# Probabilities scaled by the reciprocals of their sums on ScalarE instead of on GpSimd

## The chip, the cores and the metric

The kernel runs on one core of one Trainium2 chip. A core has five engines that run side by side, each taking its own instructions in sequence: TensorE (PE in the profile, with its weight loads as PEld), VectorE (DVE), ScalarE (ACT), GpSimd (POOL) and SyncE (SP), which here only issues transfers. They meet at semaphores. Matmuls write into PSUM, a small accumulator memory of which this kernel holds eight banks; everything else lies in on-chip memory (SBUF) or in the device's main memory. The metric is the device time of one launch in microseconds. A time is the median of several runs.

## The reference

One step of a two-layer backbone for 512 latent tokens and 128 context tokens, width 1024, in fp32. Each layer normalises and modulates its input, projects it once into four groups of heads (a short gated convolution, a chunked spatial gate, latent attention, windowed attention), projects their concatenated outputs back, adds that through a gate, and does the same for a squared-ReLU MLP. What the change touches is the softmax of both attentions of the latent tokens, cut here to its core:

```python
# latent attention, 4 heads: 512 queries on 512 + 128 keys
s = jnp.einsum('bqhd,bkhd->bhqk', q_blk, kf) * scale
p = jax.nn.softmax(s, axis=-1)
out = jnp.einsum('bhqk,bkhd->bqhd', p, v)

# windowed attention, 4 heads: a band of blocks, the context, and one sink logit per head
logits = jnp.concatenate([s_band, s_ctx, sink_column(sink, s_band)], axis=-1)
p = jax.nn.softmax(logits, axis=-1)
out = einsum(p[..., :n_band], v_band) + einsum(p[..., n_band:-1], v_ctx)
```

So each row of probabilities is an exponential divided by the sum of its row.

## The kernel before

Tokens are columns: 640 of them, worked on in two halves of 384 and 256. Nearly every matrix product is made of three fp32 matmuls (`mm3`, lines 248 to 250), because each operand is split into a rounded part and the rest: the rounded part is a ScalarE cast and the rest a VectorE subtraction (`split`, lines 253 and 254; for weights lines 239 and 240). ScalarE and VectorE therefore stand behind every operand that is computed in the kernel.

Each layer runs its projections, then windowed attention, then latent attention, then the rest of the output projection, then the MLP. Both attentions go by units of one head and two blocks of 128 queries, eight units each, and each unit has a front and a back:

- *Front of a windowed unit* (`swa_front`): score matmuls into a pair of PSUM banks; on VectorE the row's minimum with the mask (line 756); on ScalarE the exponential with its sum (line 759) and the exponential of the sink (line 761); on VectorE the addition of both (line 762) and the reciprocal (line 763); and the scaling of the probabilities `P` (line 764), on GpSimd. Widths are 384 and 512.
- *Front of a latent unit* (`mla_front`): score matmuls, the maximum on VectorE (line 996), the exponential with its sum on ScalarE (line 997), the reciprocal on VectorE (line 999), and the scaling of `Pm` (line 1000), on GpSimd. The width is 640.
- *Back* (`swa_back`, `mla_back`): TensorE transposes the scaled probabilities (line 244, tile `pt`), `split` makes `PT` or `PTm` of them, TensorE multiplies with the values (lines 793 and 1025, tile `pv`), and ScalarE, VectorE and `split` bring the result into the layer's `y`.

`pairs` writes the front of unit i+1 ahead of the back of unit i, and between the pieces of a back it draws filler from a generator: projection tiles (`fm`) in windowed attention, output tiles (`out`) in latent attention. The context tokens have small units of their own (`sc`, `pc`, `pvc`), and their transposed probabilities are copied by line 823. In the first layer VectorE also does the modulation vectors of later layers (line 174) between these pieces.

The written order is not the final one. A scheduler places the instructions on each engine by its own estimate of when each can start, so that a changed instruction also changes the order around it. Buffers come from rotating pools: two PSUM banks for `pt` and `pv`, two pairs of banks for the scores, five tiles for the probabilities.

Of the kernel before, what the change touches and what calls it, by code (L numbers as in the profile page):

```python
# [13 lines left out]
AF = mybir.ActivationFunctionType  # L14
ALU = mybir.AluOpType
# [41 lines left out]
def step_kernel(ctx, tc, xT, wf, wt, wt3, wo1, wo2, wq, wkvs, wada, wnat, wnat2, vec, rows, fnorm, cvec, cache, kpec,  # L57
                masks, rope_s, rope_q, rope_k, o_y, o_ckv, o_kpe, o_k, o_v):
    nc = tc.nc
# [27 lines left out]
    def nm(s):  # L87
        uid[0] += 1
        return f"{s}_{uid[0]}"
# [9 lines left out]
    def bank2(s="bk2"):  # L99
        return s2.tile([128, 2, 512], F32, tag="s2", name=nm(s))  # L100
# [7 lines left out]
    def tp(shape, s):  # L108
        return pool_p.tile(shape, F32, tag="p", name=nm(s))
# [136 lines left out]
    def mm3(out, lhs, rhs, start, stop, more=False):  # L246

        nc.tensor.matmul(out, lhsT=lhs[0], rhs=rhs[0], start=start, stop=False, skip_group_check=more)  # L248
        nc.tensor.matmul(out, lhsT=lhs[0], rhs=rhs[1], start=False, stop=False, skip_group_check=more)  # L249
        nc.tensor.matmul(out, lhsT=lhs[1], rhs=rhs[0], start=False, stop=stop, skip_group_check=more)  # L250
# [185 lines left out]
    def layer(l, h, next_norm, nxt):  # L436
# [165 lines left out]
        for hd in range(4):  # L602
            if hd % 2 == 0:
# [6 lines left out]
                out=u_t[:, :, d0:d0 + 64], in0=ps[:, :320].rearrange("p (t d) -> p t d", t=5),  # L610
                scalar=vl[:, V_SB + hd:V_SB + hd + 1], in1=u_t[:, :, d0:d0 + 64],
                op0=ALU.add, op1=ALU.mult)
# [122 lines left out]
        def swa_front(i):  # L735
            hq, hf = divmod(i, 2)
            n, g = divmod(hq, 2)
            r = slice(64 * n, 64 * n + 64)
            S = bank2("S")
            P = PS[i] = [tp([128, 512], "P") for _ in range(2)]  # L740
            a = sm.tile([128, 4, 2], F32, tag="as", name=nm("as"))
            for j in range(2):
                c = 2 * hf + j
                k0, kn = RNG[c]
                w = 128 * kn
                if stacked:
                    for t in (kw, kl):
                        nc.tensor.matmul(S[:, j, :w], lhsT=qw[g][:, n, 128 * c:128 * c + 128],
                                         rhs=t[:, n, 128 * k0:128 * k0 + w], start=t is kw, stop=t is kl)
                    continue  # L750
                mm3(S[:, j, :w], (qw[g][r, 0, 128 * c:128 * c + 128], qw[g][r, 1, 128 * c:128 * c + 128]),
                    (kw[r, 0, 128 * k0:128 * k0 + w], kw[r, 1, 128 * k0:128 * k0 + w]), True, True)
            for j in range(2):
                c = 2 * hf + j
                w = 128 * RNG[c][1]
                nc.vector.tensor_tensor_reduce(
                    out=P[j][:, :w], in0=S[:, j, :w], in1=msk[:, MSK[c]:MSK[c] + w], op0=ALU.add, op1=ALU.min,
                    scale=1.0, scalar=nsink[:, hq:hq + 1], accum_out=a[:, 0, j:j + 1])
                nc.scalar.activation(P[j][:, :w], P[j][:, :w], AF.Exp, scale=-1.0, bias=a[:, 0, j:j + 1],
                                     accum_out=a[:, 1, j:j + 1])  # L760
                nc.scalar.activation(a[:, 2, j:j + 1], a[:, 0, j:j + 1], AF.Exp, bias=sink[:, hq:hq + 1])
                nc.vector.tensor_add(a[:, 1, j:j + 1], a[:, 1, j:j + 1], a[:, 2, j:j + 1])
                nc.vector.reciprocal(a[:, 3, j:j + 1], a[:, 1, j:j + 1])
                nc.gpsimd.tensor_scalar(out=P[j][:, :w], in0=P[j][:, :w], scalar1=a[:, 3, j:j + 1], scalar2=1.0,
                                        op0=ALU.mult, op1=ALU.mult)
            yield

        def swa_back(i):
# [216 lines left out]
        def mla_front(i):  # L985
            hd, hf = divmod(i, 2)
            ke, qq = kk[hd % 2], qqs[hd]
            P = PS[i] = [tp([128, TOK], "Pm") for _ in range(2)]
            a = sm.tile([128, 4, 2], F32, tag="as", name=nm("as"))
            for j in range(2):  # L990
                c = 2 * hf + j
                S = bank2("S")
                for z in range(2):
                    mm3(S[:, z, :320], (qq[:, 0, 128 * c:128 * c + 128], qq[:, 1, 128 * c:128 * c + 128]),
                        (ke[:, 0, 320 * z:320 * z + 320], ke[:, 1, 320 * z:320 * z + 320]), True, True)
                nc.vector.tensor_reduce(out=a[:, 0, j:j + 1], in_=S[:, :, :320], op=ALU.max, axis=AX.XY, negate=True)
                nc.scalar.activation(P[j].rearrange("p (a b) -> p a b", a=2), S[:, :, :320], AF.Exp,
                                     bias=a[:, 0, j:j + 1], accum_out=a[:, 1, j:j + 1])
                nc.vector.reciprocal(a[:, 3, j:j + 1], a[:, 1, j:j + 1])
                nc.gpsimd.tensor_scalar(out=P[j], in0=P[j], scalar1=a[:, 3, j:j + 1], scalar2=1.0,  # L1000
                                        op0=ALU.mult, op1=ALU.mult)
                yield

        def mla_back(i):
# [78 lines left out]
        def load_up():  # L1083
# [5 lines left out]
        s_ = side()  # L1089
        next(s_)  # L1090
        pairs([swa_front(i) for i in range(7)] + [swa_ctx_front(), swa_front(7)],
              [swa_back(i) for i in range(7)] + [swa_ctx_back(), swa_back(7)], s_, C1)
        run(s_)
# [15 lines left out]
        def second():  # L1109
            run(mla_k(1))  # L1110
            run(q_pair(1))
            yield from mla_front(4)

        s_ = side2()
        pairs([mla_front(i) for i in range(4)] + [second(), mla_front(5), mla_ctx_front(), mla_front(6), mla_front(7)],
              [mla_back(i) for i in range(6)] + [mla_ctx_back(), mla_back(6), mla_back(7)], s_, C2)
        run(s_)
# [370 lines left out]
```

## Time and profile before

| | |
|---|---|
| median of 3 runs | 1513.88 us (1511.9 to 1515.99) |
| profiled execution | 1513.0 us, span 1510.8 us |
| TensorE busy | 1461.8 us, 97% |
| VectorE busy | 1133.2 us, 75% |
| ScalarE busy | 694.7 us, 46% |
| GpSimd busy | 79.3 us, 5% |
| granted TensorE clock, mean | 0.988 of full speed |

The busy shares are means over the whole span. The edited lines run in four stretches only: windowed attention at about 126 to 208 us and 865 to 940 us, latent attention at about 230 to 310 us and 962 to 1040 us. Buffer numbers are left out in the profile's names (`P`, `Pm`) and stand in the order's (`P_2104`).

### The profile page before, as it was taken

Reading aid. Unit: us, or ns where it says so; the run is one execution under the profiler, and the core shown is the slowest. Engines: PE = TensorE matmul, PEld = TensorE weight load, DVE = VectorE, ACT = ScalarE, POOL = GpSimd, SP = SyncE. Lnnn points to the kernel's source line nnn. Section 1 sums busy time; section 2 is a strip of 40 time slices with the busy share of each in tenths; the row PEclk is TensorE's granted clock in tenths of the full one; section 3 lists DMA queues with packets and bytes.
Section 4 is the critical chain, followed back from the end, with each engine's and each line's share of the span. In section 5 each row is a group of like instructions: output and inputs, shape, how many; then the busy total and the mean of one; then the engine's idle time right before and its main releaser. Section 6 shows DMA issues by size and latency. Waiting matters only on the chain.

```text
span 1510.8 us, 24974 instructions
## 1 busy us (share of the span) xinstructions
PE 1461.8 (97%) x9700; PEld 1405.1 (93%) x9700; DVE 1133.2 (75%) x2297; ACT 694.7 (46%) x1469; POOL 79.3 (5%) x103
## 2 busy tenths in 40 slices
PE   6999999999999999999999999999999999999997
PEld 3898989899999999999999998998999999999996
DVE  5998888889977867875477676887977666567656
ACT  4644556746233232233246455775826334324431
POOL 0011102200000000000000121110000000000000
PEclk9999999999999999999999999999999999999998
DMA  9643311324655444443112411022123123222312
GB/s 346 205 153 127 96 56 58 96 87 153 194 161 161 155 144 150 153 153 127 64 49 75 134 43 44 22 71 67 57 78 104 57 84 98 70 70 85 96 45 71
DMA packets 50422, 160.87 MB, mean 106 GB/s; under 512 B 6272, under 2 KB 10368, under 8 KB 50304
## 3 DMA queue, kind: packets, MB, share of 16 engines
q1 hardware_dynamic: 48320, 154.68, 31.8%
q10 hardware_dynamic: 1664, 3.93, 0.7%
q8 instruction: 77, 1.26, 0.3%
q0 software_dynamic: 320, 0.66, 0.2%
q14 instruction: 41, 0.34, 0.1%
HBM read 155.55 MB, written 3.05 MB: 105 GB/s over the span
## 4 chain that ended last, share of the span: by engine, by line
PE 81%; DVE 8%; ACT 5%; issue 2%; POOL 1%; DMA 1%; POOLq 0%; DVEq 0%; ACTq 0%
PE w L250 15%; PE w L249 15%; PE w L248 14%; PE tm L250 2%; PE tm L248 2%; PE tm L249 2%; PE qcd L248 2%; PE qcd L250 2%; PE qcd L249 2%; PE out L248 2%; PE fm L248 2%; PE fm L250 2%; PE fm L249 2%; PE out L249 2%; PE out L250 2%
## 5 line engine op out<-in xcount | busy, mean ns | idle before, releaser
L248 PE MATMUL w<-u,hl 128*128 128x384 f32 (+1 forms) x1024 | 315.8, 309 | 1.9 <-DVE x L428 1.2
L249 PE MATMUL w<-u,hl 128*128 128x384 f32 (+1 forms) x1024 | 315.9, 308 | 0.7 <-DVE u L1231 0.7
L250 PE MATMUL w<-u,hl 128*128 128x384 f32 (+1 forms) x1024 | 315.5, 309 | 0.6 <-DVE hl L240 0.6
L239 ACT CAST hl<-raw 128x1024 fp32r<-128x1024 f32 (+3 forms) x176 | 170.7, 972 | 244.0 <-PE w L250 151.4
L240 DVE TENSOR_TENSOR hl<-raw,hl 128x1024 fp32r<-128x1024 f32 (+3 forms) x176 | 199.4, 1135 | 60.6 <-ACT hl L239 59.8
L428 DVE SCALAR_TENSOR_TENSOR x<-w,mod,x 128x128 f32<-128x128 f32 (+1 forms) x384 | 155.4, 434 | 59.4 <-PE w L250 58.1
L248 PEld LDWEIGHTS w<-u,hl 128*128 128x128 f32 x1024 | 193.3, 189 | 3.0 <-DVE x L428 1.4
L249 PEld LDWEIGHTS w<-u,hl 128*128 128x128 f32 x1024 | 193.6, 189 | 1.0 <-DVE u L1231 1.0
L250 PEld LDWEIGHTS w<-u,hl 128*128 128x128 f32 x1024 | 193.4, 189 | 0.8 <-DVE hl L240 0.8
L249 PE MATMUL w<-h,hl 128*128 128x384 f32 (+1 forms) x576 | 178.8, 311 | 0.7 <-DVE h L369 0.6
L248 PE MATMUL w<-h,hl 128*128 128x384 f32 (+1 forms) x576 | 177.8, 311 | 0.4 <-ACT h L365 0.2
L250 PE MATMUL w<-h,hl 128*128 128x384 f32 (+1 forms) x576 | 178.1, 310 | 0.0
L174 DVE CUSTOM_DVE_ANT_0 junk<-adaw,cb,vec 128x1024 f32<-128x1024 f32 x84 | 108.2, 1289 | 30.6 <-DMA adaw<-in_wada 30.5
L249 PEld LDWEIGHTS w<-h,hl 128*128 128x128 f32 x576 | 109.8, 191 | 1.7 <-DVE h L369 1.5
L248 PEld LDWEIGHTS w<-h,hl 128*128 128x128 f32 x576 | 109.6, 191 | 1.4 <-ACT h L365 1.3
L250 PEld LDWEIGHTS w<-h,hl 128*128 128x128 f32 x576 | 109.8, 191 | 0.2
L174 DVE CUSTOM_DVE_ANT_0 adaw<-adaw,cb,vec 128x1024 f32<-128x1024 f32 x84 | 107.9, 1285 | 0.7
L248 PE MATMUL fm<-h,hl 128*128 128x256 f32 (+1 forms) x288 | 91.5, 318 | 0.0
L249 PE MATMUL fm<-h,hl 128*128 128x256 f32 (+1 forms) x288 | 89.7, 311 | 0.0
L250 PE MATMUL fm<-h,hl 128*128 128x256 f32 (+1 forms) x288 | 89.5, 311 | 0.0
L1176 ACT ACTIVATE rr<-w 128x384 f32<-128x384 f32 (+1 forms) x72 | 31.4, 436 | 101.5 <-PE w L250 101.4
L249 PE MATMUL tm<-hl,h 128*128 128x384 f32 (+1 forms) x240 | 77.3, 322 | 0.6 <-DVE hl L240 0.6
(338 smaller groups left out, 3237.1 us busy)
## 6 DMA issues: line engine op xcount, KB each, us to landing
raw<-in_wf SPq DMA_DIRECT2D x146, 512.0 KB, 3.5
adaw<-in_wada SPq DMA_DIRECT2D x84, 512.0 KB, 3.6
raw<-in_wo SPq DMA_DIRECT2D x24, 384.0 KB, 3.1
adan<-in_wnat SPq DMA_DIRECT2D x12, 512.0 KB, 8.2
raw<-in_wt SPq DMA_DIRECT2D x16, 384.0 KB, 4.0
x<-in_xT ACTq DMA_DIRECT2D x4, 640.0 KB, 7.1
raw<-in_wt SPq DMA_DIRECT2D x8, 288.0 KB, 2.8
raw<-in_wo SPq DMA_DIRECT2D x4, 512.0 KB, 3.6
```

Source lines behind the costliest of these rows:

```text
L174: nc.vector.tensor_tensor_reduce(out=raw if g else junk, in0=raw, in1=cb[:, g, :], op0=ALU.mult, op1=ALU.add, scale=1.0, scalar=vecs[l][:, ...
L239: nc.scalar.copy(hl[:, 0, :n], raw[:, :n])
L240: nc.vector.tensor_sub(hl[:, 1, :n], raw[:, :n], f(hl[:, 0, :n]))
L248: nc.tensor.matmul(out, lhsT=lhs[0], rhs=rhs[0], start=start, stop=False, skip_group_check=more)
L249: nc.tensor.matmul(out, lhsT=lhs[0], rhs=rhs[1], start=False, stop=False, skip_group_check=more)
L250: nc.tensor.matmul(out, lhsT=lhs[1], rhs=rhs[0], start=False, stop=stop, skip_group_check=more)
L428: nc.vector.scalar_tensor_tensor(out=x[:, m, t0:t0 + n], in0=ps[:, t0 - b0:t0 - b0 + n], scalar=mods[l][g][:, gate + m:gate + m + 1], in1= ...
L1176: nc.scalar.activation(r, ps[:, :n], AF.Relu)
```

## The change

The multiplication of the probabilities by the reciprocals of their sums becomes a ScalarE copy with a scale per partition. Nothing else is edited.

```diff
@@ swa_front
                 nc.vector.reciprocal(a[:, 3, j:j + 1], a[:, 1, j:j + 1])
-                nc.gpsimd.tensor_scalar(out=P[j][:, :w], in0=P[j][:, :w], scalar1=a[:, 3, j:j + 1], scalar2=1.0,
-                                        op0=ALU.mult, op1=ALU.mult)
+                nc.scalar.activation(P[j][:, :w], P[j][:, :w], AF.Copy, scale=a[:, 3, j:j + 1])
@@ mla_front
                 nc.vector.reciprocal(a[:, 3, j:j + 1], a[:, 1, j:j + 1])
-                nc.gpsimd.tensor_scalar(out=P[j], in0=P[j], scalar1=a[:, 3, j:j + 1], scalar2=1.0,
-                                        op0=ALU.mult, op1=ALU.mult)
+                nc.scalar.activation(P[j], P[j], AF.Copy, scale=a[:, 3, j:j + 1])
```

In the changed kernel the lines behind line 765 count one less, those behind line 1000 two less. The scheduler places instructions differently on TensorE, VectorE and ScalarE, all within the four stretches but for two transfers that change places with a neighbour. The next rows are of ScalarE at the start of windowed attention in the second layer, before; the numbers tell tiles of one name apart.

```order
L759 ACTIVATE P_9199,as_9200<-P_9199,as_9200 128x512
L761 ACTIVATE as_9200<-as_9200,row_8361 128x1
L759 ACTIVATE P_9218,as_9220<-P_9218,as_9220 128x512
L761 ACTIVATE as_9220<-as_9220,row_8361 128x1
L759 ACTIVATE P_9219,as_9220<-P_9219,as_9220 128x384
```

The same place on ScalarE after the change:

```order
L759 ACTIVATE P_9199,as_9200<-P_9199,as_9200 128x512
L761 ACTIVATE as_9200<-as_9200,row_8361 128x1
L759 ACTIVATE P_9218,as_9220<-P_9218,as_9220 128x512
L764 ACTIVATE P_9198<-P_9198,as_9200 128x384
L764 ACTIVATE P_9199<-P_9199,as_9200 128x512
L761 ACTIVATE as_9220<-as_9220,row_8361 128x1
L759 ACTIVATE P_9219,as_9220<-P_9219,as_9220 128x384
```

The two scalings of the first unit stand behind the first exponential of the second unit. ScalarE at the end of windowed attention in the first layer, before (`pc` is the context's probabilities, `sgut` the spatial gate's transposed tile):

```order
L759 ACTIVATE P_2105,as_2106<-P_2105,as_2106 128x384
L761 ACTIVATE as_2106<-as_2106,row_388 128x1
L253 CAST y_1090<-yt_2098 64x256
L823 COPY pc_2019<-ptc_2130 128x512
L684 ACTIVATE y_1086<-sgut_2138 128x384
L684 ACTIVATE y_1086<-sgut_2153 128x256
```

The same place after the change:

```order
L253 CAST y_1090<-yt_2098 64x256
L759 ACTIVATE P_2105,as_2106<-P_2105,as_2106 128x384
L761 ACTIVATE as_2106<-as_2106,row_388 128x1
L764 ACTIVATE P_2104<-P_2104,as_2106 128x512
L822 COPY pc_2019<-ptc_2130 128x512
L684 ACTIVATE y_1086<-sgut_2138 128x384
L764 ACTIVATE P_2105<-P_2105,as_2106 128x384
```

One scaling of the last unit stands ahead of the copy of the context's probabilities, the other behind it. The third place is TensorE at the end of latent attention in the first layer, before: the last two of the ten products of the last unit but one (`pv_3190`), transposes of the last unit (`pt_3209`, `pt_3216`), and output matmuls (`out_3309`) as filler.

```order
L1025 MATMUL pv_3190<-PTm_3170,vm_1097 64x256
L1025 MATMUL pv_3190<-PTm_3170,vm_1097 128x256
L244 MATMUL pt_3209<-ident,Pm_3118 128x128
L244 MATMUL pt_3209<-ident,Pm_3119 128x128
...
L248 MATMUL out_3309<-ymla_2378,hl_3292 128x384
L249 MATMUL out_3309<-ymla_2378,hl_3292 128x384
L250 MATMUL out_3309<-ymla_2378,hl_3292 128x384
L244 MATMUL pt_3216<-ident,Pm_3118 128x128
```

After the change, from the transposes of the last unit but one (`pt_3178`, `pt_3185`) on:

```order
L248 MATMUL out_3309<-ymla_2378,hl_3292 128x384
L249 MATMUL out_3309<-ymla_2378,hl_3292 128x384
L244 MATMUL pt_3178<-ident,Pm_3053 128x128
L244 MATMUL pt_3178<-ident,Pm_3054 128x128
...
L250 MATMUL out_3309<-ymla_2378,hl_3292 128x384
L244 MATMUL pt_3185<-ident,Pm_3053 128x128
L244 MATMUL pt_3185<-ident,Pm_3054 128x128
L1023 MATMUL pv_3190<-PTm_3168,vm_1097 128x256
```

The last three filler matmuls have moved ahead of the products of the last unit but one; behind them no filler is left until the end of latent attention. From the first transposes of the last unit but one (`pt_3171`) to the last unit's products stood 26 output matmuls before, and 12 stand there now.

## Rows read from the trace of the kernel before

**Rows 1.** The page: busy time by engine; the chain that ended last, by engine.
```profile
PE 1461.8 (97%) x9700; PEld 1405.1 (93%) x9700; DVE 1133.2 (75%) x2297; ACT 694.7 (46%) x1469; POOL 79.3 (5%) x103
...
PE 81%; DVE 8%; ACT 5%; issue 2%; POOL 1%; DMA 1%; POOLq 0%; DVEq 0%; ACTq 0%
```

**Rows 2.** Busy time by stretch: length, engines' us (instructions), clock, DMA share, GB/s.
```profile
126.00:208.00 82.00, 78.12 (x510) 71.88 (x511) 70.73 (x183) 44.84 (x114) 12.30 (x16) 0.96 0.29 91
230.00:310.00 80.00, 75.00 (x495) 69.07 (x494) 70.12 (x151) 52.82 (x131) 17.61 (x16) 0.98 0.24 74
865.00:940.00 75.00, 70.47 (x481) 66.62 (x480) 55.50 (x145) 43.87 (x114) 11.68 (x16) 0.97 0.15 49
962.00:1040.00 78.00, 74.62 (x504) 68.02 (x503) 63.05 (x135) 53.30 (x134) 13.40 (x16) 1.00 0.14 46
sum 315.00, PE 298.21 PEld 275.59 DVE 259.40 ACT 194.84 POOL 55.00; mean PE 74.55 PEld 68.90 DVE 64.85 ACT 48.71 POOL 13.75
```

**Rows 3.** Waits of TensorE, 108 to 312 us: total us, times, longest.
```profile
PE S L248 <- ACT Pm L997: 0.5, 1, 0.5
PE pt L244 <- POOL P L764: 0.4, 1, 0.4
...
PE pt L244 <- POOL Pm L1000: 0.2, 1, 0.2
```

**Rows 4.** Timeline of TensorE, 866 to 880 us: start, us, what [idle before <-releaser].
```profile
869.93 0.44 PE L244 MATMUL pt<-ident,P 128*128 128x128 f32 x2 [1.14 <-POOL P L764]
870.60 0.77 PE L244 MATMUL pt<-ident,P 128*128 128x128 f32 x5 [0.23 <-POOL P L764]
```

**Rows 5.** ScalarE by line and form, 108 to 312 us: busy us, mean ns.
```profile
L759 ACT ACTIVATE P<-P,as 128x512 f32<-128x512 f32 x8 | 5.7, 716 | 4.4 <-DVE as L756 4.4
L759 ACT ACTIVATE P<-P,as 128x384 f32<-128x384 f32 x8 | 4.9, 610 | 6.6 <-DVE as L756 6.5
...
L705 ACT ACTIVATE cy<-ct,vec 128x640 f32<-128x640 f32 x2 | 1.7, 839 | 0.0
```

**Rows 6.** Timeline of ScalarE, 866 to 880 us.
```profile
869.53 0.28 ACT L761 ACTIVATE as<-as,row 128x1 f32<-128x1 f32 x1
869.71 0.60 ACT L759 ACTIVATE P<-P,as 128x384 f32<-128x384 f32 x1
```

**Rows 7.** Timeline of TensorE, 126 to 147 us.
```profile
135.07 0.76 PE L244 MATMUL pt<-ident,P 128*128 128x128 f32 x5 [0.45 <-POOL P L764]
```

**Rows 8.** Timeline of ScalarE, 126 to 147 us.
```profile
132.14 0.60 ACT L759 ACTIVATE P<-P,as 128x384 f32<-128x384 f32 x1
```

**Rows 9.** Timeline of ScalarE, 200 to 206 us.
```profile
204.44 0.59 ACT L823 COPY pc<-ptc 128x512 f32<-128x512 f32 x1
```

**Rows 10.** Timeline of TensorE, 200 to 206 us.
```profile
205.08 0.66 PE L843 MATMUL pvc<-pc,vctx 128*64 128x128 f32 x8 [0.85 <-ACT pc L823]
```

**Rows 11.** Timeline of TensorE, 298 to 304 us.
```profile
298.55 1.43 PE L1025 MATMUL pv<-PTm,vm 128*128 128x256 f32 x10 [0.74 <-DVE PTm L254]
301.33 0.62 PE L248 MATMUL out<-ymla,hl 128*128 128x384 f32 x2 [1.34 <-ACT ymla L253]
...
302.07 0.34 PE L250 MATMUL out<-ymla,hl 128*128 128x384 f32 x1
302.24 0.34 PE L249 MATMUL out<-ymla,hl 128*128 128x384 f32 x1
```

**Rows 12.** Instructions of line 762: ns min/median/max, first and last start.
```profile
L762 DVE TENSOR_TENSOR as<-as x32: 138/159/608, 130.8 to 935.2; 128x1 f32<-128x1 f32 x32
```

**Rows 13.** Timeline of VectorE, 230 to 262 us.
```profile
251.16 1.49 DVE L240 TENSOR_TENSOR hl<-raw,hl 128x768 fp32r<-128x768 f32 x1
...
255.88 0.94 DVE L240 TENSOR_TENSOR hl<-raw,hl 128x768 fp32r<-128x768 f32 x1
```

**Rows 14.** Timeline of GpSimd, 230 to 262 us.
```profile
241.78 0.81 POOL L1000 TENSOR_SCALAR Pm<-Pm,as 128x640 f32<-128x640 f32 x1 [2.09 <-DVE as L999]
```

**Rows 15.** Timeline of ScalarE, 230 to 262 us.
```profile
241.22 0.20 ACT L997 ACTIVATION_READ_ACCUMULATOR Pm<-S,as 128x1 f32 x1
```

## The prediction

> **What bounds the kernel now.** I began with two lines of the page [rows 1]: TensorE is busy in 97% of the span and carries 81% of the chain that ended last; GpSimd stands for 1% of that chain. So the time is the TensorE work plus the holes in it, and GpSimd matters only where its result comes last.
>
> Then I cut out the four stretches in which the edited lines run [rows 2]: windowed attention and latent attention, once for each of the two layers. TensorE's holes there (length less busy time) are 3.9, 5.0, 4.5 and 3.4 us, 16.8 us in all. Nothing that happens in these stretches can give back more than that. ScalarE, which gets the work, is busy in 44.8 of 82, 52.8 of 80, 43.9 of 75 and 53.3 of 78 us. VectorE is the fullest engine beside TensorE, with 70.1 of 80 us in the first layer's latent attention.
>
> Third, TensorE's waits on scaled probabilities: 0.4 and 0.2 us in the first layer [rows 3], 1.14 + 0.23 us in the second [rows 4], 2.0 us in all. In the middle of a stage the transposes lie a unit behind the scaling and mostly find it done.
>
> **What the change removes and adds.** It removes 64 GpSimd instructions, 55 us [rows 2], and adds 64 on ScalarE. Their shapes stand in the trace: a scaled copy of 128x640 with a scale per partition takes 0.84 us (line 705), an exponential written over its own input 0.72 us on 128x512 and 0.61 us on 128x384 [rows 5]. So 32 x 0.84 + 16 x 0.72 + 16 x 0.61 = 26.9 + 11.5 + 9.8 = 48.2 us of durations. Consecutive ScalarE instructions overlap: one of 0.28 us starts at 869.53 and the next at 869.71 [rows 6]. Less 0.1 us each, that is 42 us of ScalarE time: some 12 us in each latent stage (65 of 80 us busy then) and 9 in each windowed one (54 of 82). ScalarE has room in the mean, and TensorE, VectorE and the DMA queues keep the work they have. What remains is order: ScalarE takes its instructions in sequence, so a scaling can hold back what stands behind it, and the scheduler has built another order from it. The terms:
>
> *First, the starts of the windowed stages.* In layer 0 TensorE waits 0.45 us at 135.07 for a scaling [rows 7]. On ScalarE the fourth exponential, at 132.14 before [rows 8], comes behind one scaling and ahead of the next: 132.14 + 0.5 + 0.7 + 0.6 = 134.0 is the end of both, so this wait goes, -0.45. In layer 1 the two scalings follow the exponential that frees the engine at 869.53 [rows 6]; they end near 870.05 and 870.7, where the transposes began at 869.93 and 870.60 [rows 4]: +0.25 with the hand-over. What stands behind on ScalarE, the copies for the next queries and the casts of the transposes, moves back some 2 us, and TensorE has projection matmuls for that. Together -0.2.
>
> *Second, the ends of the windowed stages.* The copy of the context probabilities (line 823) starts at 204.44 in layer 0 [rows 9], and TensorE waits 0.85 us for it [rows 10]. Now one scaling of 128x512 (0.62 net of the overlap) stands ahead of it, in layer 1 both (0.62 + 0.51), and in layer 0 the last transposes come 0.3 us later still. No filler stands between: +0.9 and +1.1, together +2.0.
>
> *Third, the middle of the latent stages.* Two bounds for the 24 us of added ScalarE time: below, all holes of TensorE there vanish, -8.4; above, all of it shows, +24. The nearest row is ScalarE's idle time, 27.2 and 24.7 us [rows 2], twice what is added, and fronts run a unit ahead of backs, so a late scaling meets a transpose that is later still. I take +1.0, for score matmuls that wait longer until an exponential, now behind a scaling, frees their bank; that wait is 0.5 us already [rows 3].
>
> *Fourth, the ends of the latent stages.* The new order spends its filler earlier. Between the first transposes of the last unit but one and the last product of probabilities and values stand 14 fewer output matmuls in layer 0 and 5 fewer in layer 1, at 0.17 us each from start to start, 2.4 and 0.9 us; TensorE already waits 0.74 and 1.34 us there [rows 11]. If the chain of ScalarE and VectorE ends where it did and TensorE was late anyway, nothing is lost; if TensorE comes to the end sooner in vain, 3.3 us are. I take a little under half, +1.5.
>
> *Fifth, VectorE without GpSimd beside it.* The 128x1 addition of line 762 takes 0.16 us in the median and up to 0.61 us [rows 12], a split of 128x768 1.49 us with GpSimd at work beside it and 0.94 us later, without [rows 13]. The Trainium skill (GPSIMD Engine Reference, Key points) says that GpSimd shares its interfaces to the on-chip memory with VectorE and collides with VectorE instructions that have two inputs there. These have, so the trace agrees, and by that rule alone the change is a gain. How large, the rows only bound: from nothing to 32 x 0.45 = 14 us for the additions; with the median near the least of them, some 2 us, and with a handful of splits at 0.55 us about 5 us. Hardly any of it ends in a wait of TensorE, so I count -0.5, and -0.2 for the one wait on a scaling in latent attention [rows 3].
>
> Sum: -0.2 + 2.0 + 1.0 + 1.5 - 0.5 - 0.2 = +3.6 us. The profiled execution took 1513.0 us, 1510.8 of span and 2.2 around it; the median of the runs is 0.9 higher. 1513.0 + 3.6 = 1516.6 us.
>
> **Rivals.** *ScalarE becomes the bound of latent attention (slower).* A scaling waits for a reciprocal, and on ScalarE everything queued behind it waits too: casts of transposed probabilities, on which VectorE's subtractions and TensorE's products depend. After an exponential's end at 241.42 [rows 15] GpSimd could start at 241.78 [rows 14], 0.36 us for the reciprocal and the hand-over, and more where a long VectorE instruction [rows 13] stands ahead. With 0.74 + 0.36 us each, 32 scalings take 35 of the 52 us that were idle [rows 2]; it decides as soon as casts land behind the filler of their unit. A quarter of the 35 exposed gives +9, 1522 us. For it: VectorE is nearly full there, so the two engines cannot catch up. Against it: in most places casts stand between an exponential and its scaling.
>
> *The collisions were the brake (faster).* VectorE gets back 5 us and TensorE's 2.0 us on GpSimd go; with part of that lost at the ends up to -5, 1508 us. For it: VectorE is 88% busy in the first latent stage. Against it: TensorE hardly waits there, 5.0 of 80 us [rows 2].
>
> *Nothing moves.* Scaling lies a unit ahead of its use, filler covers the ends, and the new order only shuffles: 1513.5 us. This is also the case in which the change does not do what it says: at the starts of the windowed stages two other exponentials stand between, so it is not "right behind".
>
> **How the numbers follow.** Chances: forecast 0.50, ScalarE as the bound 0.25, collisions 0.09, nothing 0.16. A measurement of this kernel can tell about 0.3% from no change, so 1509.3 to 1518.4 counts as none. Of the forecast's 0.50 I put 0.12 above 1518.4, since the second and fourth terms may both come out whole. Slower: 0.25 + 0.12 = 0.37; faster 0.09; same 0.38 + 0.16 = 0.54. The range runs from 1510 (short of the collision case) to 1524 (the larger half of the rival of 1522); the forecast's own is 1513 to 1521.
>
> **What would show it.** GpSimd at some 24 us busy and ScalarE at 737 to 743; the additions of line 762 all near 0.15 us; a wait of TensorE of 1.5 us or more on the context copy at the ends of the windowed stages; longer waits at the last products of latent attention; mid-stage holes as they are. Wrong if waits of score matmuls on exponentials, or of products on casts, grow by several us mid-stage (the first rival), or if the holes of the four stretches shrink below 14 us (the second).

## The result: slower by 0.6%, and the profile after

The changed kernel takes 1523.1 us (median of 4 runs, 1521.6 to 1525.1), the kernel before, run beside it on the same chip, 1514.9 us. The ratio is 1.0061, with a 95% interval of 1.0044 to 1.0078: some 9 us more (7 to 12), where +3.6 was forecast. The time lies inside the range, the direction is that of the forecast, the size is not. The profiled execution took 1523.4 us with a span of 1521.0, 10.2 more than that of before.

The two lines of the page answer to [rows 1]: GpSimd fell to 24 us, as written; ScalarE rose by 38 us to 733, a little less than the 737 to 743 written; VectorE's busy time fell by 4 us. Of the chain, TensorE has two points less and ScalarE one more.

```profile
PE 1464.3 (96%) x9700; PEld 1407.3 (93%) x9700; DVE 1129.1 (74%) x2297; ACT 732.8 (48%) x1533; POOL 24.2 (2%) x39
...
PE 79%; DVE 8%; ACT 6%; issue 2%; DMA 1%; POOL 0%; POOLq 0%; DVEq 0%; ACTq 0%
```

The four edited stretches by their windows (columns as in [rows 2], each stretch moved along with its stage and 1 to 3 us longer):

```profile
126.00:210.00 84.00, 80.06 (x518) 72.63 (x517) 70.00 (x183) 53.92 (x130) 0.00 (x0) 0.96 0.28 89
232.00:315.00 83.00, 76.29 (x498) 69.98 (x497) 69.14 (x152) 63.20 (x147) 0.00 (x0) 0.96 0.22 71
872.00:950.00 78.00, 70.99 (x485) 67.33 (x484) 53.70 (x144) 53.02 (x130) 0.00 (x0) 0.96 0.14 42
971.00:1050.00 79.00, 74.16 (x492) 68.21 (x490) 60.06 (x131) 62.08 (x145) 0.00 (x0) 0.98 0.14 46
```

TensorE's holes (length less busy) are 3.9, 6.7, 7.0 and 4.8 us, 22.5 in all, where [rows 2] had 16.8. They grew in layer 0's latent attention and, most of all, in layer 1's windowed attention.

TensorE's waits between 108 and 320 us answer to [rows 3]:

```profile
PE pv L1023 <- DVE PTm L254: 2.1, 3, 1.2
PE sgut L244 <- DVE as L762: 1.9, 2, 1.4
PE pt L244 <- DVE PTm L254: 1.5, 3, 1.0
...
PE pt L244 <- ACT P L764: 1.0, 1, 1.0
PE pvc L842 <- ACT pc L822: 0.7, 1, 0.7
...
PE S L248 <- ACT Pm L996: 0.4, 1, 0.4
```

The kernel before, 108 to 312 us, had of the waits for PTm, the split transposed probabilities:

```profile
PE pv L1025 <- DVE PTm L254: 0.7, 1, 0.7
...
PE pt L244 <- DVE PTm L254: 0.3, 1, 0.3
```

The score matmuls wait for exponentials as before (0.4 against 0.5 us), so the middle of the latent stage did not become worse. What grew in the latent stage are the waits for PTm, from 1.0 to 3.6 us: by 1.2 us ahead of the products of unit 7, near the stage's end, and by 1.1 in unit 3, where other waits of 0.6 us went. The waits for `sgut` stand at the end of the windowed stage, where others went in turn: the products' waits for `PT` there fell from 1.7 to 0.4 us.

VectorE's small addition came out as written (answer to [rows 12]): without GpSimd beside it, its longest is 161 ns instead of 608. The Trainium skill (GPSIMD Engine Reference, Key points) says that the two engines contend where a VectorE instruction has two inputs in the on-chip memory, as this one has, and the trace agrees. A gain in time was not seen.

```profile
L762 DVE TENSOR_TENSOR as<-as x32: 138/156/161, 131.1 to 942.2; 128x1 f32<-128x1 f32 x32
```

**The start of layer 1's windowed stage.** TensorE in the kernel after (answer to [rows 4]):

```profile
875.45 0.44 PE L244 MATMUL pt<-ident,P 128*128 128x128 f32 x2 [1.39 <-ACT P L764]
876.06 0.77 PE L244 MATMUL pt<-ident,P 128*128 128x128 f32 x5 [0.17 <-ACT P L764]
878.01 0.44 PE L248 MATMUL fm<-h,hl 128*128 128x384 f32 x1 [1.19 <-ACT fr L658]
```

and ScalarE there (answer to [rows 6]):

```profile
874.79 1.21 ACT L764 ACTIVATE P<-P,as 128x384 f32<-128x384 f32 x2
...
876.10 0.60 ACT L759 ACTIVATE P<-P,as 128x384 f32<-128x384 f32 x1
...
876.70 0.71 ACT L764 ACTIVATE P<-P,as 128x512 f32<-128x512 f32 x1
...
877.49 0.47 ACT L658 ACTIVATE fr<-fm 128x384 f32<-128x384 f32 x1
```

In the kernel before, ScalarE's copy and TensorE's next projection stood so:

```profile
870.50 0.47 ACT L658 ACTIVATE fr<-fm 128x384 f32<-128x384 f32 x1
```
```profile
871.12 0.42 PE L248 MATMUL fm<-h,hl 128*128 128x384 f32 x1
```

Count from the stage's first exponential, which starts at 867.13 before and at 872.40 after. The transposes begin 2.80 us later before and 3.05 after: +0.25, as forecast. The copy of line 658 moved from 3.37 to 5.09, behind three scalings (two in the first row, one in the third). This copy empties the bank that the next projection matmul (fm) needs, so that matmul moved from 3.99 to 5.61, with a new wait of 1.19 us.

**The last units of the latent stages.** Output matmuls are the filler there. Their busy time and count, in units 5, 6, 7 and 8 of layer 0, in the kernel before (length of the unit, then TensorE, weight load and VectorE of tile out alone, clock, DMA):

```profile
274.60:280.49 5.89, 1.62 (x6) 1.00 (x6) 1.20 (x2) 1.00 0.09 36
280.49:286.11 5.62, 1.65 (x7) 1.16 (x7) 0.00 (x0) 1.00 0.25 73
286.11:295.49 9.38, 5.78 (x26) 4.38 (x26) 1.21 (x2) 1.00 0.46 135
295.49:299.99 4.50, 0.77 (x3) 0.48 (x3) 0.00 (x0) 1.00 0.44 145
```

The same four units in the kernel after:

```profile
276.82:284.47 7.65, 3.12 (x14) 2.42 (x14) 1.21 (x2) 1.00 0.08 25
284.47:289.99 5.52, 2.58 (x11) 1.91 (x11) 0.47 (x1) 1.00 0.44 139
289.99:299.69 9.70, 4.08 (x18) 3.06 (x18) 0.74 (x2) 1.00 0.41 132
299.69:305.10 5.41, 0.00 (x0) 0.00 (x0) 0.00 (x0) 0.80 0.11 43
```

In all 42 and 43 matmuls, but 12 more of them in units 5 and 6, and eleven fewer in 7 and 8. In layer 1 the shift is smaller: 17 and 22 in units 5 and 6, 24 and 21 in 7 and 8; there too unit 8 has none left, where it had five. Why the order takes them early, ScalarE shows in unit 5, before:

```profile
275.57 0.79 ACT L997 ACTIVATE Pm<-S,as 128x640 f32<-128x640 f32 x1
...
276.90 1.08 ACT L253 CAST PTm<-pt 128x512 fp32r<-128x512 f32 x2
```

and after:

```profile
277.78 0.80 ACT L996 ACTIVATE Pm<-S,as 128x640 f32<-128x640 f32 x1
...
279.12 1.55 ACT L999 ACTIVATE Pm<-Pm,as 128x640 f32<-128x640 f32 x2
280.57 1.05 ACT L253 CAST PTm<-pt 128x512 fp32r<-128x512 f32 x2
```

Two scalings now stand between the exponential and the cast of the transposed probabilities: the cast starts 2.79 us after the exponential's start instead of 1.33. TensorE gets filler for that time, and has none when the stage ends. What it costs there is TensorE's holes in units 7 and 8, first of layer 0, then of layer 1, all instructions, before:

```profile
286.11:299.99 13.88, 12.60 (x88) 10.86 (x85) 12.10 (x24) 9.01 (x21) 3.74 (x3) 1.00 0.46 138
1019.79:1031.71 11.92, 11.07 (x78) 9.30 (x76) 8.74 (x19) 7.18 (x16) 2.17 (x2) 1.00 0.24 78
```

and after:

```profile
289.99:305.10 15.11, 11.97 (x77) 9.87 (x74) 10.04 (x21) 9.73 (x22) 0.00 (x0) 0.93 0.30 100
1026.70:1040.61 13.91, 11.29 (x80) 9.53 (x77) 9.75 (x19) 9.49 (x21) 0.00 (x0) 1.00 0.29 95
```

1.28 + 0.85 = 2.1 us before, 3.14 + 2.62 = 5.8 after: +3.6. In layer 1 they grew by 1.8 us with only three output matmuls fewer, so the count of the filler alone does not give the holes. That the later casts also lengthen the wait itself is likely; no run tells the two apart.

### The profile page after: what moved, and what is told of

The parts are those of the page before. It is cut to its first block, busy times and chain, and to the rows that moved or that the text cites. A ratio compares the mean times of both kernels' runs of the same rounds, so it can differ in the third digit from the quotient of the medians.

```text
span 1521.0 us, 24848 instructions
## 1 busy us (share of the span) xinstructions
PE 1464.3 (96%) x9700; PEld 1407.3 (93%) x9700; DVE 1129.1 (74%) x2297; ACT 732.8 (48%) x1533; POOL 24.2 (2%) x39
## 3 DMA queue, kind: packets, MB, share of 16 engines
HBM read 155.55 MB, written 3.05 MB: 104 GB/s over the span
## 4 chain that ended last, share of the span: by engine, by line
PE 79%; DVE 8%; ACT 6%; issue 2%; DMA 1%; POOL 0%; POOLq 0%; DVEq 0%; ACTq 0%
PE w L250 14%; PE w L249 14%; PE w L248 13%; PE tm L250 2%; PE tm L248 2%; PE tm L249 2%; PE fm L248 2%; PE qcd L248 2%; PE fm L250 2%; PE fm L249 2%; PE qcd L250 2%; PE qcd L249 2%; PE out L248 2%; PE out L249 2%; PE out L250 2%
## 5 line engine op out<-in xcount | busy, mean ns | idle before, releaser
L253 ACT CAST hl<-s 128x1024 fp32r<-128x1024 f32 x28 | 29.3, 1047 | 104.4 <-PE w L250 73.8
```

The source lines that it names most:

```text
L253: nc.scalar.copy(h_out, src)
```

## The experiments

All were timed in five rounds beside the kernel before. A thousandth of the ratio is 1.5 us. Two places of each profiled execution are set beside the ratios. *Start* runs from the first rb matmul (the norm's sum) of the layer's attention half to the end of unit 1's value products, in the kernel before from 772.88 to 876.37 us. *Holes* are TensorE's in units 7 and 8 of both layers, worked out as above.

| kernel | ratio to before, 95% interval | start of layer 1, us | holes, us |
|---|---|---|---|
| before | | 103.5 | 2.1 |
| the change | 1.0061 [1.0044, 1.0078] | 105.0 | 5.8 |
| e1 windowed scalings only | 1.0025 [1.0011, 1.0040] | 107.8 | |
| e2 latent scalings only | 1.0023 [1.0013, 1.0034] | 103.5 | 5.7 |
| e3 unread copies on ScalarE | 1.0038 [1.0024, 1.0052] | 103.4 | 4.4 |
| e4 change, casts on GpSimd | 1.0028 [1.0013, 1.0043] | 107.9 | 4.2 |
| e5 before, casts on GpSimd | 1.0003 [0.9991, 1.0015] | 103.3 | |
| e6 as e1, less layer 1's start | 1.0002 [0.9992, 1.0011] | 103.3 | |
| e7 layer 0's start only | 0.9996 [0.9983, 1.0008] | 103.4 | |
| e8 latent units 1 to 4 only | 0.9992 [0.9982, 1.0002] | 103.4 | 2.4 |
| e9 as e1, q copies on VectorE | 1.0010 [0.9993, 1.0028] | 102.9 | |
| e10 latent units 5 to 8 only | 1.0021 [1.0007, 1.0035] | 103.4 | 5.0 |
| e11 e7 and e8 together | 1.0000 [0.9987, 1.0012] | 103.4 | |
| e12 change, less two places | 1.0007 [0.9995, 1.0020] | 103.4 | |

**Halves of the change.** e1 has only the first hunk of the diff, e2 only the second.

> The scaling moves to ScalarE in windowed attention alone; latent attention keeps GpSimd. Theory A (ScalarE's sequence: each added instruction pushes back what is queued behind it, and this shows where TensorE has no filler left) and the two traces expect a gain of 1.9 us at the start of the first windowed stage, a loss of 1.7 us at the start of the second and of 2.1 us at their ends: +2 us, ratio 1.001 to 1.002. If the two parts do not add up (theory C, the order over the whole layer decides), it lies elsewhere, above +4 us or below -1.

> The scaling moves to ScalarE in latent attention alone. From the two traces the latent stages lose 2.3 us in the first layer and 3.1 us in the second: all theories expect +5 to +6 us, ratio 1.0035 to 1.004, if the parts add up; with the windowed part the whole is +8. The waits of the products on casts and subtractions should be those of the changed kernel, 2 us and 1.7 us by layer.

Measured: e1 1.0025, a little over what was expected; e2 1.0023, under it, with waits of the products of 2.1 and 1.7 us, as expected. Each costs 3.5 to 4 us. In e1's trace the start of layer 1 has the same two waits as the change, but another price behind them:

```profile
871.44 0.44 PE L244 MATMUL pt<-ident,P 128*128 128x128 f32 x2 [1.40 <-ACT P L764]
...
874.01 0.69 PE L248 MATMUL fm<-h,hl 128*128 128x384 f32 x1 [1.19 <-ACT fr L658]
874.50 0.52 PE L249 MATMUL fm<-h,hl 128*128 128x384 f32 x1
874.82 0.52 PE L250 MATMUL fm<-h,hl 128*128 128x384 f32 x1
```

After the second wait the matmuls come 0.32 us apart instead of the 0.17 of the kernel before, until 879.6: the lower of the two clock levels. From 870 to 880 us the granted clock (the third number from the end) is 1.00 in the change and 0.66 in e1, in this order:

```profile
870.00:880.00 10.00, 7.09 (x43) 6.03 (x43) 6.57 (x22) 8.09 (x23) 0.00 (x0) 1.00 0.12 46
870.00:880.00 10.00, 7.23 (x27) 6.72 (x27) 7.00 (x19) 7.88 (x19) 0.00 (x0) 0.66 0.00 0
```

So the same two waits cost 1.5 us in the change's execution and 4.3 in e1's.

**ScalarE's time, or the probabilities' lateness?** e3 leaves all scalings on GpSimd and adds, behind each latent one, a copy of the same size on ScalarE that nothing reads:

```
 nc.gpsimd.tensor_scalar(out=P[j], in0=P[j], ...)
+nc.scalar.activation(msk[:, :TOK], cb[:, 0, :TOK], AF.Copy, scale=a[:, 3, j:j + 1])
```

> Latent attention keeps the scaling on GpSimd, and ScalarE makes, in the place of the scaling and behind the same reciprocal, a scaled copy of the same width from another tile into a tile that nobody reads. Theory A (time in ScalarE's sequence): as the latent part alone, +5 to +6 us. Theory B (the scaled probabilities come later, since the scaling waits for its turn on ScalarE): as the kernel before, 0 to +1 us, because the probabilities are as early as there.

1.0038: theory B is out. The time on ScalarE alone costs at least as much as e2's scalings, although the probabilities come from GpSimd as before. The holes of units 7 and 8 grew less than in e2 (4.4 against 5.7 us), but e3 has the rest earlier: from the end of unit 1 to the end of unit 8, TensorE's holes in both layers are 4.2 us before, 7.7 in e2 and 7.6 in e3. What e3 lost beyond e2 (2 us) may be the clock's, by the estimate of the last section; it lies within the intervals.

e4 gives ScalarE room again; e5 is its control without the change:

```
-nc.scalar.copy(hl[:, 0, :n], raw[:, :n])
+(nc.gpsimd.tensor_copy if pool else nc.scalar.copy)(hl[:, 0, :n], raw[:, :n])   # pool: n == 768
```

> The changed kernel, with the rounding casts of the eight output weight units per layer that serve as filler in latent attention moved from ScalarE to GpSimd: 16 x 0.84 = 13 us less on ScalarE, half of what the change added to latent attention, on instructions that are loaded ahead. Theory A: half or more of the latent loss comes back, 3 to 5 us under the changed kernel, 1.002 to 1.004 of before. Theories B and C: as the changed kernel, 1.005 to 1.006.

> The kernel before, with only the casts of the 768-wide output weights moved from ScalarE to GpSimd; scalings stay on GpSimd. It is the control of e4 (which had these casts on GpSimd beside the change, at 1.0028 against 1.0061 of the change). Theory A (ScalarE's own queue in the latent stages is what the change overfills, and the casts only made room again): here the room is not needed, so 0.998 to 1.001. Rival (the casts on ScalarE cost time whatever stands beside them, and e4 gained for that reason alone): 1513.9 - 5 = 1510, ratio 0.996 to 0.997. Third (GpSimd now has casts in front of scalings that wait): slower, 1.001 to 1.004.

e4 1.0028 against the change's 1.0061, e5 1.0003: the casts themselves cost nothing that shows, the room does count. In e4 layer 1 has output matmuls in its last unit again (3, where the change has 0) and 1.15 us of holes in units 7 and 8; layer 0 still has 3.0. From unit 1 to unit 8 the holes are 5.4 us, where the change has 7.8.

**Where in the windowed stages?** e6 is e1 with `if l == 0 or i > 1:` ahead of the ScalarE line, GpSimd's otherwise; e7 has `if l == 0 and i < 2:`.

> Scalings of the windowed stages on ScalarE as in e1, but the first two units of layer 1 (8 of 32 windowed tiles) stay on GpSimd; latent scalings stay on GpSimd. Theory A1 (most of the windowed loss is the start of layer 1, where the q copy behind the scalings holds the projection's bank and TensorE falls to the lower clock; the traces of the change and of e1 show 1.65 and 4.3 us there): the start of layer 1 comes back to the 103.5 us of before and the ratio falls from 1.0025 to between 0.998 and 1.001. Rival A2 (the loss is in the ends and middles of the windowed stages, spread over all 16 units): three quarters of it stay, 1.0015 to 1.0025, and the start's increment alone does not carry the total.

> Only the first two units of layer 0's windowed stage (4 scalings) on ScalarE, all others on GpSimd. In the change's trace the start of layer 0 was 1.85 us shorter. Theory (that gain is a true one: the first transposes wait for a scaling of about 0.7 us instead of 1.2 to 1.7 us and nothing is queued behind): ratio 0.998 to 0.9995, about 1.5 us faster. Rival (the start only jitters by 3 us between executions, and the gain is given back at the next unit): 1.000 within 0.001.

e6: 1.0002, and the start is back at 103.3. A windowed unit has two scalings, so those that stay on GpSimd are four (the expectation says eight): four scalings of 32 carry most of the windowed loss. e7: 0.9996; its interval holds no change, so the gain at layer 0's start is not shown.

e9 tests the cause at that place. All windowed scalings stay on ScalarE, and in layer 1 the three copies of the second q projection go to VectorE, away from them:

```
+if l == 1 and i == 1:
+    nc.vector.tensor_scalar(out=raw[:, 0:384], in0=pss[0][:, 0:384], scalar1=sc, ...)   # and lines 659, 660
+else:
     nc.scalar.activation(raw[:, 0:384], pss[0][:, 0:384], AF.Copy, scale=sc)
```

> As e1 (all windowed scalings on ScalarE, latent ones on GpSimd), but in layer 1 the three copies that empty the second q projection's banks (lines 658 to 660) run on VectorE instead of ScalarE, so that no scaling stands ahead of them. e6 showed that the windowed loss lies at the start of layer 1 (1.0002 without it, 1.0025 with it). Theory Q (the loss there is these copies standing behind scalings, which holds the projection's bank): the wait of 1.19 us for line 658 goes or falls under 0.5 us, the start's increment goes from 107.8 back to 103 to 104.5 us, ratio 0.999 to 1.001. Rival P (the loss is the first transposes' wait for scaled probabilities, 1.4 us there, with the fall of the clock behind it): the 1.19 us wait may go but the increment stays at 105 or more and the ratio at 1.0015 to 1.0025. Rival V (VectorE, which was busy 9 of 10 us there, now delays the maxima): a new wait on VectorE of about 1 us, 1.001 to 1.003.

The start is 102.9, under that of before. TensorE in e9's trace takes the projection first and then finds the probabilities ready:

```profile
872.80 0.45 PE L248 MATMUL fm<-h,hl 128*128 128x384 f32 x1 [0.91 <-DVE fr L659]
873.28 0.44 PE L244 MATMUL pt<-ident,P 128*128 128x128 f32 x2
```

Two waits of 1.40 and 1.19 us in e1 became one of 0.91: theory Q for the place, with a wait left that is above the half microsecond expected. Since the order took the projection first, the transposes' own wait went too, so e9 does not tell the two waits apart; in the change's trace the first is 0.25 us longer than before and the second is new. The ratio, 1.0010, is too wide (0.9993 to 1.0028) to say more.

**Where in the latent stages?** e8 has `if i < 4:` ahead of the ScalarE line, e10 `if i >= 4:`.

> Scalings of latent units 1 to 4 of each layer on ScalarE (16 of 32), units 5 to 8 and the windowed stages on GpSimd. Theory A (ScalarE is overfull only in the second half, where the context's exponentials and the casts of output weights join; the trace of the change shows it busy from 276 to 297 us with one break of 0.57 us): almost nothing is lost, ratio 0.999 to 1.001 against 1.0023 with all 32. Rival B2 (each scaling on ScalarE delays the next exponential by 0.83 us wherever it stands): half of the loss, 1.001 to 1.0015. Rival C2 (the loss is in the first half, the tail only shifts): all of it, 1.002 or more.

> Scalings of latent units 5 to 8 of each layer on ScalarE, units 1 to 4 and the windowed stages on GpSimd: the counterpart of e8 (0.9992). Theory A (ScalarE is overfull in the second half; the casts of transposed probabilities come late and the value products wait for them): the whole loss of e2 is here, ratio 1.002 to 1.004, waits of value products and transposes for PTm of 3 to 3.6 us in the stretch 255 to 316 us as in e2 (before 1.0). Rival (the loss needs both halves, a backlog that is built up from the first unit on): 1.000 to 1.001 and waits near those of before.

0.9992 and 1.0021: the whole loss is in the second half. TensorE's holes in units 7 and 8 tell them apart, in e8

```profile
288.93:302.81 13.88, 12.58 (x87) 10.82 (x85) 12.11 (x24) 9.03 (x21) 3.73 (x3) 1.00 0.46 138
1018.39:1031.25 12.86, 11.79 (x84) 10.20 (x81) 9.22 (x19) 8.01 (x19) 1.60 (x2) 1.00 0.23 73
```

1.3 and 1.1 us, and in e10

```profile
287.72:301.90 14.18, 11.05 (x76) 9.03 (x74) 10.03 (x21) 9.73 (x22) 0.00 (x0) 1.00 0.35 108
1019.41:1033.27 13.86, 11.99 (x79) 9.35 (x76) 9.69 (x21) 10.21 (x23) 0.00 (x0) 1.00 0.22 67
```

3.1 and 1.9. Output matmuls in unit 8 are 3 and 4 in e8 (before 3 and 5), none in either layer of e10. The waits for PTm that e10's expectation named (3 to 3.6 us in layer 0) came out at 2.4: they are part of the holes, not the measure of them.

**Together.** e11 has the conditions of e7 and e8; e12 those of e6 and e8, which is the change without the two places.

> Layer 0's first two windowed units (4 scalings) and latent units 1 to 4 of each layer (16 scalings) on ScalarE, the other 44 on GpSimd: e7 and e8 together. If what they measured is real and adds up (0.9996 and 0.9992): 0.9988, between 0.998 and 0.9998, about 1.8 us under the kernel before. If both were only scatter about no change: 0.9995 to 1.0005.

> The change, except at the two places that the runs before point to: the first two windowed units of layer 1 (8 scalings) and latent units 5 to 8 of each layer (16) stay on GpSimd; the other 40 of 64 scalings are on ScalarE. If the two places carry the loss of the change (1.0061), as e6 (1.0002 for the windowed rest) and e8 (0.9992 for the latent rest) say, and the rest adds up: 0.9985 to 1.0005. If the parts hinder each other (e1 and e2 add up to 1.0048, under the change's 1.0061): 1.001 to 1.0025.

e11: 1.0000. No version faster than the kernel before was found; what e7 and e8 seemed to gain was within their scatter. e12: 1.0007, above what was expected, but its interval reaches down to 0.9995. With 44 of 64 scalings on ScalarE (not 40, for the reason given at e6) it loses about 1 us, at most 3 by its interval, and the 20 others carry some 8 of the change's 9.

## Why the prediction was wrong in size

**First term, the step that failed.** "What stands behind on ScalarE, the copies for the next queries and the casts of the transposes, moves back some 2 us, and TensorE has projection matmuls for that." The copy did move back 1.7 us. The cover was not there: the next projection matmul waits for that very copy, since it empties the bank. Forecast for layer 1: +0.25. Measured: e1 less e6, 0.0023 or 3.5 us (by the two intervals about 1 to 6), with 1.5 (the change) to 4.3 us (e1) in single executions, by whether the clock fell behind the wait. For layer 0, -0.45 was forecast; the transposes' wait there is 1.0 us instead of 0.4, and e7 shows no sure gain.

**Second term, the ends of the windowed stages, +2.0.** The wait of 1.5 us or more on the context copy came in layer 1 alone, 2.20 us where there was none:

```profile
944.55 1.12 PE L842 MATMUL pvc<-pc,vctx 128*64 128x128 f32 x8 [2.20 <-ACT pc L822]
```

But the kernel before waited just ahead of it, for the gate's transposes:

```profile
934.38 0.52 PE L244 MATMUL sgut<-ident,u 128*128 128x128 f32 x3 [1.40 <-DVE as L762]
935.42 0.66 PE L244 MATMUL sgut<-ident,u 128*128 128x128 f32 x2 [0.52 <-DVE y L685]
```

After the change 0.70 us of these 1.92 is left, so much of the new wait stands in their place. From the end of unit 6's products to the end of the context's (`pvc`), layer 1 takes 13.3 to 13.8 us in the six profiled executions with this end on ScalarE and 11.9 to 12.8 in the eight others: about 1.3 us. In layer 0 the wait is 0.7 instead of 0.85 [rows 10], so the mechanism failed there. e6 and e12, which keep both ends on ScalarE, allow for it 1.7 and 3.0 us by their intervals. So the traces show about 1.3 of the 2.0, and no run measures it alone.

**Third term, the middle of the latent stages, +1.0.** Nothing: e8's 0.9992, the score matmuls' wait as it was, and holes in units 5 and 6 of both layers of 0.65 us before and 0.25 after.

**Fourth term, the ends of the latent stages, +1.5.** The mechanism was right, filler spent early and missing at the end, and the size was off. The holes of units 7 and 8 grew by 3.6 us, and e2 and e10 measured 3.5 and 3.2, about the upper bound of 3.3. "If the chain of ScalarE and VectorE ends where it did and TensorE was late anyway" was the argument for taking less than half; neither held: the casts come 1.5 us later in unit 5, and with no filler in unit 8 TensorE stands waiting. That the filler ran out is read from the traces; that time in ScalarE's sequence is the cause, e3 and e4 show.

**Fifth term, -0.5 and -0.2.** The additions of line 762 did what was written, and VectorE's busy time fell by 4 us; a gain in time was not seen.

So the sum by experiments: 3.5 at layer 1's start, 3.5 at the latent ends, 0 to 3 for the rest, 7 to 10 us against 9 measured (7 to 12). e1 and e2 add up to 1.0048, short of 1.0061, but within the intervals.

**The rivals.** ScalarE as the bound (1522) came nearest in time. Its seed was right: two scalings stand ahead of the casts of transposed probabilities (e3: time on ScalarE is enough). But it did not bound the stage; TensorE had filler in units 5 and 6 and paid later, and the nearness of 1522 is luck: its 9 us were to come from the latent stages, which lost some 3.5. Collisions as the brake fell with e2, slower though the latent scalings had left GpSimd, and with e8 and e11, which gained nothing sure. "Nothing" fell with the ratio.

## What to carry over

Before work is put on an in-order engine with idle time, list what stands behind it that hands a bank back to TensorE: a copy out of a bank is worth its delay, even where TensorE seems to have other matmuls, if those need the same banks. Count filler as a stock: where a delay is covered by filler, ask whether any is left at the end of the stage, and price the end by at least the whole of the missing filler. A mean share of idle time (ScalarE's 27 of 80 us) says nothing about either.

## What the runs showed of the hardware

The price of one wait varies with the clock. The layer's end, from the last value products of the latent stage to the next rb matmul, takes 11.7 to 12.3 us in 15 of the 28 layer ends; in the other 13 it takes 13.3 to 14.7 (14 profiled executions, that of before among them). In the kernel before, layer 1:

```profile
1031.00:1044.00 13.00, 10.76 (x62) 9.06 (x59) 9.38 (x19) 4.97 (x10) 0.00 (x0) 1.00 0.00 0
```

and in e9, where the scalings of this stage are on GpSimd too, after the same waits of 0.8 and 1.3 us:

```profile
1035.00:1050.00 15.00, 12.96 (x57) 11.42 (x56) 9.66 (x20) 4.97 (x10) 0.00 (x0) 0.77 0.00 0
```

A granted clock of 0.77 instead of 1.00 makes TensorE busy longer with no more work, 2.4 us here (14.7 against 12.3). So one profiled execution can't tell 3 us, and the ratios stand beside each trace above. e9's own span, 1516.6 us, holds these 2.4 us; the stage is not one that its edit touches.

The clock has a part in the change's loss too. Every run has its span and its mean granted clock on record; one less the clock, times the span, is an estimate of what the lower level cost, if TensorE was busy in it throughout. By that the four runs of the change lost 20 us to the clock (16.7 to 22.8), and the runs of the kernel before, in the four sets beside the experiments, 16.4 to 17.4 in the mean. So some 3 of the change's 9 us may be the clock's; 6 are left, near the 5.7 by which the holes of the four stretches grew. By the same estimate e1 less the clock is +2.5 us, e2 +3.7 and e3 +3.8. Four runs are few, and no run here sets the clock apart from the waits that go before its fall.
